# Where the weight sums of two matrices are made: block sums of w_out and w_proj_a moved into the recurrence and the attention

## The chip, the cores and the metric

The kernel runs on one core of a Trainium2 chip (8 cores, two dies of four). A core has five engines that run side by side, each with its own instruction queue: TensorE (PE) for matrix products, VectorE (DVE), ScalarE (ACT), GpSimd (POOL), and SyncE (SP), which here only issues transfers. Transfers (DMAs) are issued from the queues of SP, ACT and POOL and are carried out by 16 DMA engines. The metric is the device time of one execution in microseconds (us), lower is better.

## The reference

One decoder layer on 512 tokens of 1024 channels, float32, with two parallel branches:

```python
h = rms_norm(x, norm_g)
proj = h @ w_in                       # columns: recurrence q, f, i, gate z_a | attention c_q, c_kv, rope key, gate z_b | merge logits
y_a = hgrn2_branch(hq, hf, hi, hz, lower_bounds, hg_norm_g)     # gated linear recurrence, 8 heads of 128, chunks of 32
y_b = mla_branch(cq, ckv, kr, mz, q_a_g, w_uq, kv_a_g, w_ukv)   # latent attention, causal, 8 heads
gates = sigmoid(glog + b_gate)        # two gates of 1024 channels
merged = gates[0] * (y_a @ w_proj_a) + gates[1] * (y_b @ w_proj_b)
x = x + merged @ w_out
return rms_norm(x, final_norm_g)
```

## The kernel before

**Products.** Every float32 operand is split into a high part (a cast, on ACT) and the rest (a subtraction, on DVE), and a product is three matmuls: high by high, high by low, low by high. Weights come in blocks of 128 x 1024 numbers (512 KB): `load_w` issues the transfer on SP into one of three `w_raw` slots (L112), ACT casts it to `w_hi` (L118), DVE subtracts to `w_lo` (L119), four slots each. A transfer can only be issued when its slot is free, so SP waits for the `w_lo` of three blocks before.

**Strassen products.** The two merge gates (columns of `w_in`), `w_proj_a` and `w_out` are multiplied by a Strassen scheme with seven block products in place of eight. It needs four sums of 512 x 512 blocks of the weight. They are made by the DMA engines in DRAM by the class `BlockSums`: for each of the four sums, `start` queues two copies of 512 KB from the matrix into a DRAM tensor (`g_t`, `pa_t`, `out_t`; L751), and `add(n)` adds a second block to sum n by two accumulating DMAs on POOL's queue (L758). Sums 1 and 3 (`add(1)`, `add(3)`) add one of these tensors to another. `sum(n)` loads a finished sum through `load_w`, `block(i, j)` loads a block of the matrix itself.

The queued copies are not issued at once. Each `load_w` transfer that SP issues takes one copy from the list `queued` and issues it right behind itself. The adds on POOL are tied to POOL's work: `step()` takes the next entry of the list `adds` and places it behind POOL's latest instruction.

**Stages.** (1) norm of x, latent projections; (2) the recurrence, four pairs of heads (`hg_pair`), two or three calls of `step()` in a pair; (3) the attention, eight heads: scores, softmax (POOL scales the rows, L699), transposes on PE (L715), values; every second head there is a rotary exchange (`mla_turn`), in which ACT's queue moves rows between partitions by DMA (`qs<-qr`, L628 and L635) and POOL multiplies (L629 to L631); (4) the first merge gate by Strassen (`strassen`, matmuls L849), whose first two products run in head 7, then the second gate, then `w_proj_a`; (5) `w_proj_b` in four chunks of 256 columns; (6) `w_out` by Strassen (L1045), the residual sum, the final norm and the store.

Before the change, `start` is called for the two gates and `w_proj_a` ahead of the recurrence, and for `w_out` ahead of stage 4's remaining five products. The adds of `w_proj_a` are placed in heads 2 (two sums), 4 and 6, those of `w_out` behind the first gate's product. POOL also fetches there the stored sums of h (`s<-h`, L950), eight DMAs of 512 KB.

The order of instructions is made by a scheduler on all engines, except where `manual_schedule` keeps the written order: on PE in the Strassen products, and on PE, DVE and ACT in stage 6. The last Strassen product of `w_out` uses sum 4 (`t4`), which is loaded through `w_raw` and split into the tiles of sum 1 (`t_hl[0]`) once these are free.

Of the kernel before, what the change touches and what calls it, by code (L numbers as in the profile page):

```python
# [38 lines left out]
def hybrid_layer(ctx: ExitStack, tc: tile.TileContext, a):  # L39
    nc = tc.nc  # L40
# [117 lines left out]
    def split(hi, lo, src):  # L158

        nc.scalar.copy(hi, src)  # L160
        nc.vector.tensor_tensor(lo, src, hi.bitcast(F32), op=ALU.subtract)  # L161
# [460 lines left out]
    def mla_turn(pair):  # L622

        ps = low(load_w(w_uq[:, :, 2 * pair : 2 * pair + 2, 128:192]), 0, 3)
        qr, qs = ma_pool.tile([P, S], F32, "qr"), ma_pool.tile([P, S], F32, "qs")
        nc.scalar.copy(qr[:], ps[:])
        for b in range(4):
            nc.scalar.dma_start(qs[32 * b : 32 * b + 32, :], qr[32 * (b ^ 1) : 32 * (b ^ 1) + 32, :])  # L628
        nc.gpsimd.tensor_tensor(qr[:], qr[:], qtab[:, 0], op=ALU.mult)  # L629
        nc.gpsimd.tensor_tensor(qs[:], qs[:], qtab[:, 1], op=ALU.mult)  # L630
        nc.gpsimd.tensor_tensor(qr[:], qr[:], qs[:], op=ALU.add)  # L631

        qx = ma_pool.tile([P, S], F32, "qs")
        for i in range(2):
            nc.scalar.dma_start(qx[64 * i : 64 * i + 64, :], qr[64 - 64 * i : 128 - 64 * i, :])  # L635
        return qr, qx

    def mla_rope(qr, qx):

        qp, qh = [ma_pool.tile([P, S], F32R, f"qp{i}") for i in range(2)], ma_pool.tile([P, S], F32R, "qh")  # L640
        nc.scalar.copy(qh[:], qx[:])
        for i in range(2):
            own, other = slice(64 * i, 64 * i + 64), slice(64 - 64 * i, 128 - 64 * i)
            nc.scalar.copy(qp[i][own], qr[own])
            nc.vector.tensor_tensor(qp[i][other], qx[other], qh[other].bitcast(F32), op=ALU.subtract)
        return qp
# [34 lines left out]
    def mla_scores(h, pool, qn, kn, qp, final=False):  # L681

        pn = []
        for i in range(NT):
            n = (i + 1) * P
            bl = slice(i * P, n)
            sps = ax_tile()
            qh = qp[h % 2]
            mm3(sps[:, :n], qn, kn, (slice(None), bl), (slice(None), slice(0, n)), True, False)
            for x in range(2):  # L690
                nc.tensor.matmul(sps[:, :n], qh[:, bl], kpe[x][:, :n], start=False, stop=x == 1)  # L691
            sm = pool.tile([P, 4], F32, "sm", 4)
            p = pool.tile([P, n], F32, f"p{i}")
            nc.vector.tensor_tensor(sps[:, bl], sps[:, bl], mask_inf[:], op=ALU.add)
            nc.vector.tensor_reduce(sm[:, 0:1], sps[:, :n], axis=AX.X, op=ALU.max, negate=True)
            nc.vector.tensor_scalar(sm[:, 1:2], sm[:, 0:1], SCALE, None, op0=ALU.mult)  # L696
            nc.scalar.activation(p[:, :n], sps[:, :n], AF.Exp, scale=SCALE, bias=sm[:, 1:2], accum_out=sm[:, 2:3])  # L697
            nc.vector.reciprocal(sm[:, 3:4], sm[:, 2:3])
            scaled_p = (nc.vector if final else nc.gpsimd).tensor_scalar(p[:, :n], p[:, :n], sm[:, 3:4], 0.5,  # L699
                                                                         op0=ALU.mult, op1=ALU.mult)  # L700
            if not final:
                last_pool[0] = scaled_p
            pn.append(p)
        return pn
# [23 lines left out]
    kh = [slice(0, 2), slice(2, 4)]  # L728
# [40 lines left out]
    gate_w = [BlockSums(f"g{b}", w_in[:, COL_G + b * D : COL_G + b * D + D]) for b in range(2)]  # L769
    pa_w = BlockSums("pa", a["w_proj_a"][0])  # L770
    out_w = BlockSums("out", a["w_out"][0])
    h_dram = [[dram.tile([P, 4, 256], F32, name=f"h{n}{i}") for i in range(2)] for n in range(1, 5)]

    def early_sums(q):
# [9 lines left out]
        def keep(n, tag, src):  # L784
# [13 lines left out]
        keep(4, "qn", e12)  # L798

    adds = [(gate_w[0], 0), (gate_w[0], 2), (gate_w[1], 0), (gate_w[0], 1), (gate_w[1], 2), (gate_w[0], 3), (gate_w[1], 1),  # L800
            None, (gate_w[1], 3)]

    def step():
        if adds and last_pool[0]:
            x = adds.pop(0)
            if x:
                x[0].add(x[1])

    for w in (*gate_w, pa_w):
        w.start()  # L810

    for pair in range(H // 2 - 1):
# [93 lines left out]
    yb = ybp.tile([P, H, S], F32, "yb")  # L906
    qp, nope, pn = early
    late = None
    for h in range(H):
        pools = (ma_pool, mw)  # L910
        if h % 2 and h + 1 < H:
            turned_q = mla_turn((h + 1) // 2)
        if h:
            pn = mla_scores(h, pools[h % 2], *nope, qp, h + 1 == H)
        if h % 2 and h + 1 < H:
            qp = mla_rope(*turned_q)
        if h:
            z = mla_gate(h)
        if h:
            if h + 1 < H:  # L920
                nope = mla_nope(h + 1, pools[(h + 1) % 2])
            mla_out(*late)
            if h % 4 == 0:
                v = mla_values(h)
        hook = lambda: mla_transpose(pn)
        if h + 1 == H:
            with tc.manual_schedule(engines={mybir.EngineType.PE}):
                pts, later = [], []
                w11, w21 = gate_w[0].block(0, 0), gate_w[0].block(1, 0)
                u = ch_product(w11, h11, copied("c11", 1.0))  # L930
                ch_product(w21, h12, lambda b, ps: later.append((b, ps)), tile=mm_tile, hook=lambda: pts.extend(hook()))
                mla_out(h, pts, v, z)
        elif h:
            late = (h, hook(), v, z)
            if h % 2 == 0:
                pa_w.add(*{2: (0, 2), 4: (1,), 6: (3,)}[h])
        else:
            with tc.manual_schedule(engines={mybir.EngineType.PE}):
                nope = mla_nope(1, pools[1])
                v = mla_values(0)  # L940
                late = (0, hook(), v, z)
# [25 lines left out]
        closed("c11", 0, 0, 1.0, gate_out(0, lambda j: ma[:, j]))(b, ps)  # L967
    h_ops = (h11, h12, h22, s1, s2, s3, s4)
    y11, y12, y21, y22 = blocks(ya)
    out_w.start()  # L970
    with tc.manual_schedule(engines={mybir.EngineType.PE}):
        strassen(gate_w[0], h_ops, gate_out(0, lambda j: ma[:, j]), gp, first=u,
                 between={3: lambda: a_parts(y11, q1), 4: lambda: a_parts(y12, q2), 5: lambda: a_parts(y22, q3),
                          6: lambda: [minus(y22[:, q], y22[:, q], y21[:, q]) for q in kh]})
    out_w.add(0, 2)
    out_w.add(1)
    out_w.add(3)
    g1 = {j: z_tile()[:] for j in (0, 1, 4)}
    for n, j in enumerate((2, 3, 5, 6, 7)):
        g1[j] = g_rows[:, n]  # L980
# [28 lines left out]
    m_bot = [m2p.tile([P, 4, S], F32R, f"m_bot{i}") for i in range(2)]  # L1009
    t_hl = [[m2p.tile([P, 4, 512], F32R, f"t{n}{i}") for i in range(2)] for n in (1, 2)]  # L1010
    a11, a12, a21, a22 = blocks(ma)
    xr = [ya[:, 2 * t : 2 * t + 2].rearrange("p k c -> p (k c)") for t in range(NT)]
    for n, c in enumerate((0, 2, 1, 3)):
        for i, ps in enumerate(proj_ch(a["w_proj_b"][0], c * 256, ybs)):
            j = 2 * c + i
            g = g1[j]
            nc.vector.scalar_tensor_tensor(g, g, 1.0, ps[:], op0=ALU.add, op1=ALU.mult)
            nc.vector.tensor_tensor(ma[:, j], ma[:, j], g, op=ALU.add)
            if j < 4:
                split(m_top[0][:, j], m_top[1][:, j], ma[:, j, 0:256])  # L1020
            else:
                split(m_bot[0][:, j - 4], m_bot[1][:, j - 4], ma[:, j])
        if n == 1:
            t1 = out_w.sum(1, t_hl[0])
        elif n == 2:
            t2 = out_w.sum(2, t_hl[1])
            with tc.issue_after(last_dma[0].ins):
                for t in range(NT):
                    xr_in = nc.sync.dma_start(xr[t], a["x"][0, t * P : t * P + P, :])
    gp.close()  # L1030


# [106 lines left out]
    with tc.manual_schedule(engines={mybir.EngineType.PE, mybir.EngineType.DVE, mybir.EngineType.Activation}):  # L1139
        for q in kh:  # L1140
            minus(a22[:, q], a22[:, q], a21[:, q])
            split(s1[0][:, q], s1[1][:, q], a22[:, q])
        for q in kh:
            minus_minus(a22[:, q], a22[:, q], a11[:, q])
            split(s2[0][:, q], s2[1][:, q], a22[:, q])
        u = product(m_top, 0, w11, lambda t, ps: add_to(t, 0, ps), by_tile=False)
        for q in kh:
            minus_minus(a12[:, q], a12[:, q], a22[:, q])
        w22 = out_w.block(1, 1)
        product(m_bot, 0, w21, row11, tile=mm_tile, by_tile=False)  # L1150
        for q in kh:
            minus(a21[:, q], a11[:, q], a21[:, q])
        a_parts(a21, m_top)
        r = product(s1, 0, t1, lambda t, ps: add_to(t + 2, 1, ps), by_tile=False)
        a_parts(a12, s1)
        t3 = out_w.sum(3)
        product(s2, 0, t2, lambda t, ps: add_to(t, 1, ps), u, by_tile=False)
        t4 = out_w.sum(4, t_hl[0])
        product(s1, 0, w22, row12, r)
        product(m_top, 0, t3, row22, u)  # L1160
        last_product(m_bot, 2, t4, u, row21)
# [44 lines left out]
```

## Time and profile before

| | |
|---|---|
| three runs | 643.65, 645.54, 647.35 us; median 645.54 |
| profiled execution | 642.71 us; span from first to last instruction 640.8 us |
| PE busy | 609.8 us, 95% of the span |
| DVE, ACT, POOL busy | 433.1, 285.6, 147.0 us |
| mean granted clock of PE | 0.982 |
| moved by DMA | 114.37 MB, 178 GB/s in the mean |

In the groups of the profile, `out<-in` names the tile written and the tiles read, L is the line of the kernel, and x the count. In PE's, DVE's, ACT's and POOL's rows of the timeline the first number is the start in us from the span's start, the second the time of the row, and a bracket at the end tells how long the engine had been idle before it and what it waited for. "SPq" and "POOLq" stand for a queue that issues DMAs; the time of such a row is that of issuing, not of moving.

### The profile page before, as it was taken

What the parts mean: (1) busy time and instruction counts of PE and PEld (TensorE: products, weight loads), DVE (VectorE), ACT (ScalarE), POOL (GpSimd) and SP (SyncE); (2) the same over time, 40 slices, a digit from 0 to 9 for tenths busy, and PEclk for the clock granted to TensorE, in tenths of its full rate; (3) what the DMA queues carried; (4) which work ended last, traced back from release to release, by engine and by line L of the source; (5) the groups of instructions that cost most, each with busy time, mean ns of one, the idle gap of its engine ahead of it and who ended that gap; (6) DMA issues with size and microseconds to landing.
All of it is one profiled execution on the core that took longest, in us unless ns stands there. A gap on an engine that the chain in (4) does not pass through costs nothing.

```text
span 640.8 us, 9797 instructions
## 1 busy us (share of the span) xinstructions
PE 609.8 (95%) x3688; PEld 533.7 (83%) x3688; DVE 433.1 (68%) x679; ACT 285.6 (45%) x531; POOL 147.0 (23%) x245
## 2 busy tenths in 40 slices
PE   8999999999999999999989999947799999999994
PEld 5998888888888888888878888947799999888883
DVE  7727989498945479675767667523467777667785
ACT  5554343333233333355445545342467864333352
POOL 3106322535422045113441142401100000000002
PEclk9999999999999999999999999987899999999999
DMA  7549399969695523504393825999976555685123
GB/s 258 165 139 339 115 296 339 265 180 218 197 210 125 142 71 86 134 16 117 74 192 77 177 82 131 344 278 255 209 225 187 181 192 174 194 319 147 59 98 132
DMA packets 74799, 114.37 MB, mean 178 GB/s; under 512 B 7512, under 2 KB 41726, under 8 KB 74752
## 3 DMA queue, kind: packets, MB, share of 16 engines
q1 hardware_dynamic: 65100, 89.69, 44.1%
q0 software_dynamic: 7952, 21.50, 17.8%
q10 hardware_dynamic: 1700, 2.56, 1.4%
q8 instruction: 29, 0.48, 0.3%
q14 instruction: 18, 0.15, 0.1%
HBM read 105.34 MB, written 39.85 MB: 227 GB/s over the span
## 4 chain that ended last, share of the span: by engine, by line
PE 80%; DMA 7%; DVE 5%; ACT 3%; issue 2%; POOL 2%; ACTq 1%; POOLq 0%; DVEq 0%
PE mm_ps L91 17%; PE mm_ps L92 17%; PE mm_ps L93 17%; PE ax_ps L849 14%; DMA w_raw<-w_in 3%; PE mm_ps L849 3%; DMA w_raw<-g_t 2%; DMA qs<-qr 2%; PE mm_ps L271 1%; PE ax_ps L691 1%; DVE w_lo L119 1%; PE ax_ps L541 1%; PE ax_ps L715 1%; PE ax_ps L236 1%; PE ax_ps L503 1%
## 5 line engine op out<-in xcount | busy, mean ns | idle before, releaser
L119 DVE TENSOR_TENSOR w_lo<-w_raw,w_hi 128x1024 fp32r<-128x1024 f32 (+3 forms) x116 | 138.4, 1204 | 109.0 <-ACT w_hi L118 103.1
L118 ACT CAST w_hi<-w_raw 128x1024 fp32r<-128x1024 f32 (+3 forms) x116 | 115.4, 1005 | 168.9 <-PE mm_ps L92 75.5
L91 PE MATMUL mm_ps<-hT,w_hi 128*128 128x512 f32 x320 | 125.7, 394 | 0.3 <-DVE qn L161 0.3
L92 PE MATMUL mm_ps<-hT,w_hi 128*128 128x512 f32 x320 | 125.1, 391 | 0.0
L93 PE MATMUL mm_ps<-hT,w_lo 128*128 128x512 f32 x320 | 124.7, 392 | 0.0
L849 PE MATMUL ax_ps<-s,w_hi 128*128 128x256 f32 x384 | 59.8, 301 | 16.0 <-ACT w_hi L118 16.0
L91 PEld LDWEIGHTS mm_ps<-hT,w_hi 128*128 128x128 f32 x320 | 60.1, 188 | 12.3 <-DVE qn L161 0.6
L93 PEld LDWEIGHTS mm_ps<-hT,w_lo 128*128 128x128 f32 x320 | 60.1, 188 | 12.3
L92 PEld LDWEIGHTS mm_ps<-hT,w_hi 128*128 128x128 f32 x320 | 60.1, 188 | 11.8
L849 PEld LDWEIGHTS ax_ps<-s,w_hi 128*128 128x128 f32 x384 | 54.6, 209 | 16.8 <-ACT w_hi L118 16.8
L93 PE MATMUL mm_ps<-w_hi,hT 128*128 128x512 f32 (+1 forms) x96 | 36.6, 383 | 0.0
L92 PE MATMUL mm_ps<-w_lo,hT 128*128 128x512 f32 (+1 forms) x96 | 36.5, 382 | 0.0
L91 PE MATMUL mm_ps<-w_hi,hT 128*128 128x512 f32 (+1 forms) x96 | 36.4, 386 | 0.0
L1096 POOL TENSOR_SCALAR ssum<-ssum 128x1 f32<-128x1 f32 x3 | 0.9, 310 | 154.3 <-ACT sq L1083 154.3
L849 PE MATMUL ax_ps<-s,w_lo 128*128 128x256 f32 x192 | 33.2, 297 | 0.0
L699 POOL TENSOR_SCALAR p<-p,sm 128x128 f32<-128x128 f32 (+3 forms) x28 | 15.2, 545 | 65.5 <-DVE sm L696 33.2
L849 PEld LDWEIGHTS ax_ps<-s,w_lo 128*128 128x128 f32 x192 | 28.6, 206 | 0.2 <-DVE w_lo L119 0.2
L697 ACT ACTIVATE p<-ax_ps,sm 128x128 f32<-128x128 f32 (+3 forms) x32 | 16.9, 529 | 25.6 <-DVE sm L696 23.3
L460 DVE RECIPROCAL tf<-pr 128x512 f32<-128x512 f32 x8 | 26.8, 3349 | 0.2
L91 PE MATMUL mm_ps<-cT,w_hi 128*128 128x512 f32 x52 | 20.7, 398 | 0.0
L93 PEld LDWEIGHTS mm_ps<-w_hi,hT 128*128 128x128 f32 x96 | 18.0, 188 | 3.0
L91 PEld LDWEIGHTS mm_ps<-w_hi,hT 128*128 128x128 f32 x96 | 18.0, 188 | 3.0
(296 smaller groups left out, 1207.8 us busy)
## 6 DMA issues: line engine op xcount, KB each, us to landing
w_raw<-w_in SPq DMA_DIRECT2D x54, 512.0 KB, 5.5
g_t<-w_in SPq DMA_DIRECT2D x16, 512.0 KB, 8.6
w_raw<-g_t SPq DMA_DIRECT2D x16, 512.0 KB, 4.7
g_t<-w_in POOLq DMA_DIRECT2D x8, 512.0 KB, 9.9
pa_t<-w_proj_a SPq DMA_DIRECT2D x8, 512.0 KB, 12.9
g_t<-g_t POOLq DMA_DIRECT2D x8, 512.0 KB, 10.2
out_t<-w_out SPq DMA_DIRECT2D x8, 512.0 KB, 17.3
s<-h POOLq DMA_DIRECT2D x8, 512.0 KB, 10.5
```

The lines of the kernel that those rows point to most:

```text
L91: nc.tensor.matmul(ps, lh[lsl], rh[rsl], start=start, stop=False)
L92: nc.tensor.matmul(ps, lh[lsl], rl[rsl], start=False, stop=False)
L93: nc.tensor.matmul(ps, ll[lsl], rh[rsl], start=False, stop=stop)
L118: last_hi[0] = nc.scalar.copy(hi[:, :o], raw[:, :o])
L119: last_lo[0] = nc.vector.tensor_tensor(lo[:, :o], raw[:, :o], hi[:, :o].bitcast(F32), op=ALU.subtract)
L236: nc.tensor.matmul(idle[:], zero[:, :P], zero[:], start=True, stop=True)
L271: nc.tensor.matmul(ps, hT[l][:, 4 * kh + k, t * P : t * P + P], c_hl[kh][r][:, k * 256 : k * 256 + 256], start=kh == 0 and kind == 0 and k ...
L460: nc.vector.reciprocal(rp[:], pr[:])
L503: nc.tensor.matmul(sps[:, sl], kt_[:, sl], v_sb[i][:, (h % 4) * P : (h % 4) * P + P], start=True, stop=True)
L697: nc.scalar.activation(p[:, :n], sps[:, :n], AF.Exp, scale=SCALE, bias=sm[:, 1:2], accum_out=sm[:, 2:3])
L699: scaled_p = (nc.vector if final else nc.gpsimd).tensor_scalar(p[:, :n], p[:, :n], sm[:, 3:4], 0.5, op0=ALU.mult, op1=ALU.mult)
L849: nc.tensor.matmul(ps[:, o], w[k // 2][i][:, k % 2, cols], ap[j][:, k], start=not banks and c == 0 and n == 0, stop=n == 11, skip_group_ch ...
```

## The change

```diff
     adds = [(gate_w[0], 0), (gate_w[0], 2), (gate_w[1], 0), (gate_w[0], 1), (gate_w[1], 2), (gate_w[0], 3), (gate_w[1], 1),
-            None, (gate_w[1], 3)]
+            (pa_w, 0), (gate_w[1], 3), (pa_w, 2), None, (pa_w, 1), (out_w, 0), (pa_w, 3), (out_w, 2), (out_w, 1), (out_w, 3)]
...
-    for w in (*gate_w, pa_w):
+    for w in (*gate_w, pa_w, out_w):
         w.start()
...
             late = (h, hook(), v, z)
-            if h % 2 == 0:
-                pa_w.add(*{2: (0, 2), 4: (1,), 6: (3,)}[h])
+            step()
...
-    out_w.start()
     with tc.manual_schedule(engines={mybir.EngineType.PE}):
         strassen(gate_w[0], h_ops, gate_out(0, lambda j: ma[:, j]), gp, first=u,
...
-    out_w.add(0, 2)
-    out_w.add(1)
-    out_w.add(3)
...
+    t4_raw = yb[:, 4:8]
...
                     xr_in = nc.sync.dma_start(xr[t], a["x"][0, t * P : t * P + P, :])
+                for q in kh:
+                    xr_in = nc.sync.dma_start(t4_raw[:, q], out_w.t[3][:, q])
...
-        t4 = out_w.sum(4, t_hl[0])
+        t4 = [[t[:, q] for t in t_hl[0]] for q in kh]
+        for hl, q in zip(t4, kh):
+            split(*hl, t4_raw[:, q])
```

Three things change. The copies of `w_out` are queued with the others ahead of the recurrence, so that they come out behind loads of head pairs 2 and 3. The adds of `w_proj_a` and `w_out` go into the list of `step()`, one sum at a time: two in pairs 2 and 3, and one in each of heads 1 to 6, where `step()` is now called. Sum 4 of `w_out` is no longer loaded through the `w_raw` slots near the end, but by two DMAs into the upper half of `yb`, the second branch's output, which is read for the last time in stage 4; they are issued in stage 5 behind the loads of x.

How this moves instructions is shown at three places. First SP, in head pairs 2 and 3, as a piece of the difference (`pa_t_658` is the last of w_proj_a's four tensors, `out_t_659` and `out_t_660` the first two of w_out's):

```order
 L751 DMA pa_t_658<-w_proj_a 128x2x512
-L112 DMA w_raw<-w_in 128x4x256 x2
+L112 DMA w_raw<-w_in 128x4x256
+L751 DMA out_t_659<-w_out 128x2x512
+L112 DMA w_raw<-w_in 128x4x256
+L751 DMA out_t_659<-w_out 128x2x512
 L110 DMA w_raw<-w_uq 128x2x64 x3
-L112 DMA w_raw<-w_in 128x4x256 x6
+L112 DMA w_raw<-w_in 128x4x256
+L751 DMA out_t_660<-w_out 128x2x512
```

Each of eight loads there now has a copy of w_out behind it; the same eight copies are gone from behind the loads of the first gate.

Second POOL, in heads 4 to 6. Before:

```order
L699 TENSOR_SCALAR p_3522<-p_3522,sm 128x512
L758 DMA pa_t_656<-pa_t_655 128x1024 x2
L699 TENSOR_SCALAR p_3719<-p_3719,sm 128x128
L699 TENSOR_SCALAR p_3733<-p_3733,sm 128x256
L699 TENSOR_SCALAR p_3747<-p_3747,sm 128x384
L629 TENSOR_TENSOR qr<-qr,qtab 128x512
L630 TENSOR_TENSOR qs<-qs,qtab 128x512
L699 TENSOR_SCALAR p_3761<-p_3761,sm 128x512
L631 TENSOR_TENSOR qr<-qr,qs 128x512
L699 TENSOR_SCALAR p_3888<-p_3888,sm 128x128
```

And with the change:

```order
L699 TENSOR_SCALAR p_3536<-p_3536,sm 128x512
L758 DMA out_t_661<-w_out 128x2x512 x2
L699 TENSOR_SCALAR p_3733<-p_3733,sm 128x128
L699 TENSOR_SCALAR p_3747<-p_3747,sm 128x256
L699 TENSOR_SCALAR p_3761<-p_3761,sm 128x384
L699 TENSOR_SCALAR p_3775<-p_3775,sm 128x512
L758 DMA out_t_660<-out_t_659 128x1024 x2
L629 TENSOR_TENSOR qr<-qr,qtab 128x512
L630 TENSOR_TENSOR qs<-qs,qtab 128x512
L631 TENSOR_TENSOR qr<-qr,qs 128x512
L699 TENSOR_SCALAR p_3904<-p_3904,sm 128x128
```

Head 4's sum is now one of w_out, head 5 has a sum of its own ahead of the rotary products, and its last scaling has moved ahead of them.

Third ACT, in the first gate (`part` is the copy of a product's banks, `q` a part of the recurrence's output that is split there). Before:

```order
L160 CAST q_4342<-ya 128x512 x2
L865 ACTIVATE part<-ax_ps 128x512 x2
L118 CAST w_hi<-w_raw 128x1024 x2
L160 CAST q_4344<-ya 128x512 x2
L118 CAST w_hi<-w_raw 128x1024
L865 ACTIVATE part<-ax_ps 128x512
L118 CAST w_hi<-w_raw 128x1024
```

And with the change:

```order
L160 CAST q_4358<-ya 128x512 x2
L865 ACTIVATE part<-ax_ps 128x512
L118 CAST w_hi<-w_raw 128x1024 x2
L160 CAST q_4360<-ya 128x512 x2
L865 ACTIVATE part<-ax_ps 128x512
L118 CAST w_hi<-w_raw 128x1024 x2
L160 CAST q_4362<-ya 128x512 x2
```

The casts of the next product's two blocks stood behind both copies of the banks; now they stand between the two.

## The prediction

> **What bounds the kernel now.** I read the page first, then the stages by windows, the idle gaps of TensorE (PE) row by row, the chain of waits, and last the transfers.
>
> ```profile
> span 640.8 us, 9797 instructions
> ...
> PE   8999999999999999999989999947799999999994
> ...
> PEclk9999999999999999999999999987899999999999
> ```
>
> One slice is 16 us. PE is full nearly everywhere, except for the last slice and a dip (4, 7, 7) at slices 27 to 29, from 416 us on; there the granted clock dips too. Stage by stage (from:to, length, busy us of PE, PEld, DVE, ACT, POOL, then clock, share of the DMA engines, GB/s):
>
> ```profile
> 80.00:120.00 40.00, 40.00 (x266) 33.70 (x266) 30.47 (x46) 17.13 (x37) 10.59 (x9) 1.00 1.01 314
> 160.00:230.00 70.00, 70.00 (x445) 59.54 (x438) 40.21 (x52) 24.06 (x57) 21.97 (x33) 1.00 0.66 160
> 230.00:400.00 170.00, 166.68 (x932) 142.15 (x931) 121.14 (x250) 78.95 (x175) 51.11 (x77) 1.00 0.46 107
> 421.77:463.60 41.83, 25.04 (x145) 24.06 (x145) 14.22 (x17) 13.76 (x20) 5.61 (x6) 0.76 1.01 248
> 480.00:540.00 60.00, 60.00 (x503) 60.00 (x502) 44.04 (x56) 42.47 (x64) 0.00 (x0) 1.00 0.57 186
> ```
>
> The fourth row is the first merge gate's Strassen product, the fifth the same kind of work for the second gate and w_proj_a. There PE does 503 matmuls in 60 us, 119 ns each, with the DMA engines at 0.57. In the fourth row three products of 48 matmuls need 41.83 us, and the DMA engines are full (1.01). PE's own rows show the gaps, with what ended each in brackets:
>
> ```profile
> 421.13 0.64 PE L849 MATMUL ax_ps<-s,w_lo 128*128 128x256 f32 x4
> 423.39 0.50 PE L849 MATMUL ax_ps<-s,w_hi 128*128 128x256 f32 x2 [1.62 <-ACT w_hi L118]
> 431.32 1.65 PE L849 MATMUL ax_ps<-s,w_hi 128*128 128x256 f32 x6 [7.43 <-ACT w_hi L118]
> ...
> 444.14 1.65 PE L849 MATMUL ax_ps<-s,w_hi 128*128 128x256 f32 x6 [4.49 <-ACT w_hi L118]
> ...
> 455.26 0.98 PE L849 MATMUL ax_ps<-s,w_hi 128*128 128x256 f32 x6 [2.42 <-ACT w_hi L118]
> ...
> 463.60 1.18 PE L849 MATMUL ax_ps<-hT,w_hi 128*128 128x256 f32 x8 [0.79 <-DVE part L872]
> ```
>
> PE waits for the cast of a weight block; the chain says what the cast waited for:
>
> ```profile
> 424.62 18.34 DMA w_raw<-w_in
> 443.04 1.05 ACT w_hi L118
> 445.37 15.08 DMA w_raw<-g_t
> ```
>
> So two loads set the end of this stage. The transfers of 421 to 464 us and, below, of 480 to 540 us (count, size, median us to landing):
>
> ```profile
> out_t<-out_t POOLq DMA_DIRECT2D x4, 512.0 KB, 9.6
> w_raw<-g_t SPq DMA_DIRECT2D x4, 512.0 KB, 12.4
> w_raw<-w_in SPq DMA_DIRECT2D x3, 512.0 KB, 13.7
> out_t<-w_out SPq DMA_DIRECT2D x3, 512.0 KB, 18.0
> ...
> w_raw<-g_t SPq DMA_DIRECT2D x4, 512.0 KB, 4.2
> ```
>
> The same load takes 12.4 us beside the copies and sums of w_out, and 4.2 us without them. A block of 24 matmuls lasts 2.9 us on PE and there are three raw slots, so landing, the cast of 1.05 and the subtraction after it, about as long, must fit into 8.6 us: with 4.2 they do, with 12.4 they don't.
>
> **Part 1: the eight copies and eight sums of w_out leave the first gate.** Without late loads the three products take 3 x 48 x 0.12 = 17.28 us. The stage loses 41.83 - 17.28 = 24.55 us: 16.79 idle, and 25.04 - 17.28 = 7.76 of matmuls at the lower clock. Both go when the loads are on time. The order of ACT supports it: the two casts of the second product stood behind both copies of the first one's banks (the 1.62 us gap), and now stand between them. Bounds of what remains: nothing, or the whole 1.62 us plus its share of slow clock; the load issued last before the stage stays close to its need, so I take half, 0.8. Gain 23.7 us.
>
> The slow part can be weighed. "TensorE: Matmul & The Clock Gate" of the Trainium skill (Part 1: The HAM clock gate) says that an idle window of about 3.4 us halves PE's clock and about 3.4 us of sustained work restores it. Three gaps would by that cost at most 3 x 1.7 = 5.1 us, and the sum would be 2.7 us smaller; the 7.76 us of the rows decide.
>
> **Part 2: the copies now ride behind the loads of head pairs 2 and 3, from about 164 us.** Each adds 512 KB read and written. I cost this at nothing: from 80 to 120 us such copies already run, the engines are as full as in the bad stage (1.01), and PE is busy 40.00 of 40.00: a block's 24 matmuls on 512 columns last 5.3 us there (0.22 us each, by the row 565:575 in part 4), against 2.9 in the gates. Where they go the share is 0.66. If the cover were gone, rival D has the price.
>
> **Part 3: the sums, one at a time.** Two of w_proj_a's go to pair 2 and 3, the others and w_out's four go one to each of heads 1 to 6. Each is two DMAs on POOL's queue, in front of the softmax scalings (L699) that PE's transposes (L715) wait for.
>
> ```profile
> 315.88 4.70 POOL L758 DMA_DIRECT2D pa_t<-w_proj_a  x4
> ...
> 344.00 0.37 POOL L699 TENSOR_SCALAR p<-p,sm 128x128 f32<-128x128 f32 x1 [8.10 <-DVE sm L698]
> ...
> 352.07 1.70 POOL L758 DMA_DIRECT2D pa_t<-pa_t  x2
> ...
> 373.07 2.25 POOL L631 TENSOR_TENSOR qr<-qr,qs 128x512 f32<-128x512 f32 x1
> 387.03 0.37 POOL L699 TENSOR_SCALAR p<-p,sm 128x128 f32<-128x128 f32 x1 [11.71 <-DVE sm L696]
> ...
> PE ax_ps L715 <- POOL p L699: 2.4, 2, 1.6
> ```
>
> Head 2 issues two DMAs (2.4 us) where it issued four (4.70). Head 3's fall into idle time of 8.10 us. Head 4 pays 2.4 for 1.70. Head 5's 1.70 stands ahead of the rotary products (L629 to L631), with 11.71 us idle behind them. No sum waits for an unfinished one: each comes at least a head after what it reads, some 21 us here (387.03 - 344.00 is two heads), against 9.6 us of landing. So 0, between a gain of the 2.4 us that PE waits there now and a loss as large.
>
> **Part 4: the last block's sum goes to the yb tile early.** Its two loads no longer hold ACT and DVE at the end:
>
> ```profile
> 620.28 1.05 ACT L118 CAST t<-w_raw 128x1024 fp32r<-128x1024 f32 x1 [4.09 <-DMA w_raw<-out_t]
> ...
> 627.34 5.87 PE L1045 MATMUL ax_ps<-t,m_bot 128*128 128x512 f32 x36 [0.93 <-DVE ya L1079]
> ...
> 547.18 0.40 PE L91 MATMUL mm_ps<-hT,w_hi 128*128 128x512 f32 x1
> ...
> 565.00:575.00 10.00, 10.00 (x45) 8.28 (x45) 5.98 (x9) 1.97 (x3) 0.00 (x0) 1.00 1.02 378
> ...
> 576.12 1.05 ACT L118 CAST w_hi<-w_raw 128x1024 fp32r<-128x1024 f32 x1 [3.96 <-DMA w_raw<-w_proj_b]
> ```
>
> DVE stands in order, so the late second half pushes the row sums behind it, and PE's last product waits 0.93 us for one; that goes, and since only that product's own epilogue follows, the end moves with it. Bounds: 0 and 0.93. The price is 1 MB more at 565 us, at 378 GB/s 2.8 us, ahead of w_proj_b's last two loads. Their cast moves from 576.1 to about 579; PE reaches them after three chunks of 48 matmuls at 10.00/45 = 0.22 us and 24 short ones, 547.2 + 32.0 + 2.9 = 582 us. Covered; uncovered it would cost up to 2.8.
>
> **Sum.** 23.7 + 0 + 0 + 0.9 = 24.6 us. The profiled execution took 642.71 us, 1.9 more than its span, so it would take 618.1. It lies 2.8 us under the median of the runs, 645.54; from that, 621 us is my forecast.
>
> **Rivals.**
>
> B, half of the stall stays. The loads into the first gate also run beside the fetch of the h sums. Those of 385 to 421 us landed like this:
>
> ```profile
> L112 SPq DMA_DIRECT2D w_raw<-g_t x4: 327/334/347, 390.6 to 416.0; - x4
> ...
> DMA to landing us min/median/max: 4.4/9.3/14.2
> ```
>
> If two loads stay 9.3 - 4.2 = 5.1 us late, 10.2 us of idle and, at 7.76/16.79, 4.7 of slow clock remain: 621 + 14 = 635. Against it: the engines stay full through all of 421 to 464 us, and the list of that time shows no such fetch.
>
> C, the sums disturb the rotary exchange. Its hops, ACT's DMAs qs<-qr, lie on the chain:
>
> ```profile
> 289.33 3.50 DMA qs<-qr
> ...
> 323.18 6.17 DMA qs<-qr
> ```
>
> The second ran beside four sums, the first beside none. If each of the three exchanges has both hops 2.7 us longer and PE pays all, 16 us come back: 637. For it: more sums lie in the attention now, twelve DMAs for eight; "DMA: Bandwidth & Descriptors" of the Trainium skill (Issuing engines are not separate DMA queues) says that transfers of every engine share the same 16 and interleave, and these two rows agree. Against it: PE idles only 3.3 us in all of 230 to 400 us (third row of the windows), with eight such DMAs, and head 2 loses two.
>
> D, slower: SP's queue is held by the copies in pair 2 and 3. Loads queue behind them on SP, and one copy's issue already took long (the first row: least, median and most ns of one):
>
> ```profile
> L751 SPq DMA_DIRECT2D pa_t<-w_proj_a x8: 564/686/10022, 109.4 to 154.0; - x8
> ...
> 187.09 26.04 SPq L112 DMA_DIRECT2D w_raw<-w_in  x6
> ...
> 198.12 1.05 ACT L118 CAST w_hi<-w_raw 128x1024 fp32r<-128x1024 f32 x1 [1.84 <-PE mm_ps L92]
> ```
>
> If all eight take 10.02 us against PE's 5.3 per block, PE falls 8 x 4.7 = 38 us behind. A load's lead, from its issue to the cast that waits only for PE, covers 198.1 - 187.1 - 4.2 = 6.8; 31 us are lost for 24.6 gained: 652. It decides from (24.6 + 6.8)/8 + 5.3 = 9.2 us per copy. Against it: w_proj_a's eight took 0.7 us in the median, and PE never stopped.
>
> That the scheduler leaves the copies where they were is excluded by the order.
>
> **How the numbers follow.** Forecast 0.72; B 0.12; C 0.08; B and C together, near 649 and with any cushion about where it was, 0.03; D 0.05. 0.5% is 3.2 us, about what a measurement of this kernel can tell from no change. Faster: 0.72 + 0.12 + 0.08 = 0.92; within 0.03; slower 0.05. The likeliest case alone runs from 645.5 - 24.55 - 0.93 - 2.4 = 617.7, less 1.9 of spread in the runs, to 621 + 1.6 + 0.9 + 2.4 + 2.8 = 629. Leaving out no more than 2 in 10, the range is 615 to 634.
>
> **What would show it.** In the changed profile: part 1 is right if the three products between the first and the last of the gate take under 20 us at clock 1.00, with loads landing in 4 to 6 us; part 2 if PE stays full from 160 to 230 us; part 3 if PE's idle time from 230 to 400 us stays under 6 us; part 4 if the last product no longer waits. Loads landing above 9 us in the first gate without any copy beside them would make part 1 wrong, a gap of PE between 164 and 250 us part 2.

## The result, and the profile after

The changed kernel takes 622.74 us in the median of four runs (621.24 to 625.46), the kernel before in the same comparison 644.6 us (640.87 to 647.35): a ratio of 0.967, 95% interval 0.961 to 0.973. Forecast were 621.0 us and a range of 615 to 634. The profiled execution took 623.33 us against 642.71 before, 19.4 us less, where the sum of the prediction's terms was 24.6. The total is near; but one of its terms is larger than what the whole gained, and two that were put at nothing took 5.7 us back.

The page of the changed kernel (span, then PE and the granted clock in 40 slices of 15.5 us):

```profile
span 621.4 us, 9796 instructions
...
PE   8999999999999998999998999999999999999995
...
PEclk9999999999999998999999999999999999999998
```

The dip of slices 27 to 29 is gone; the granted clock has a new, small one in slice 16, at 245 us (told under The clock). The stages by windows of the changed kernel (length, busy PE, PEld, DVE, ACT, POOL, clock, share of the DMA engines, GB/s); the third row holds the gate's three products that took 41.83 us before:

```profile
160.00:230.00 70.00, 70.00 (x452) 59.58 (x446) 39.09 (x50) 22.32 (x54) 20.75 (x32) 1.00 0.82 219
230.00:400.00 170.00, 164.49 (x905) 139.41 (x904) 116.45 (x238) 77.47 (x170) 61.21 (x87) 0.99 0.58 124
427.48:445.76 18.28, 17.79 (x146) 17.38 (x145) 14.63 (x17) 12.61 (x20) 0.00 (x0) 1.00 0.67 208
480.00:540.00 60.00, 60.00 (x472) 58.63 (x471) 43.25 (x58) 35.13 (x50) 0.00 (x0) 1.00 0.58 182
```

The loads issued in those 18 us (count, size, median us to landing):

```profile
w_raw<-w_in SPq DMA_DIRECT2D x4, 512.0 KB, 4.9
w_raw<-g_t SPq DMA_DIRECT2D x4, 512.0 KB, 4.9
```

PE's own rows, with what it waited for in brackets: in pair 3 of the recurrence, the last scores of pair 3 (L517), the gate's first product, two waits in the gate, and the last product of w_out:

```profile
244.25 0.50 PE L91 MATMUL mm_ps<-hT,w_hi 128*128 128x512 f32 x1 [1.99 <-DVE z L563]
...
263.34 0.86 PE L517 MATMUL ax_ps<-qi,ki 128*64 128x64 f32 x22
...
407.19 1.16 PE L849 MATMUL ax_ps<-hT,w_hi 128*128 128x256 f32 x8
...
428.13 0.98 PE L849 MATMUL ax_ps<-s,w_hi 128*128 128x256 f32 x6 [0.25 <-ACT w_hi L118]
...
429.58 0.51 PE L849 MATMUL ax_ps<-s,w_lo 128*128 128x256 f32 x2 [0.24 <-DVE w_lo L119]
...
608.36 5.78 PE L1043 MATMUL ax_ps<-t,m_bot 128*128 128x512 f32 x36
```

With five landmarks of PE the 19.4 us are placed: the start of the last scores of pair 2 and of pair 3 (L517), of the first gate's first product and of the product of its last sum (the rows `ax_ps<-hT` of L849), and of the last product of w_out. Each row of the table ends at the landmark that it names.

| stretch | before | after | difference | prediction |
|---|---|---|---|---|
| start to pair 2's scores | 211.19 | 211.33 | +0.14 | 0 |
| to pair 3's scores (259.29; 263.34) | 48.10 | 52.01 | +3.91 | 0 |
| to the first gate (401.31; 407.19) | 142.02 | 143.85 | +1.83 | 0 |
| to the product of the gate's last sum (463.60; 445.76) | 62.29 | 38.57 | -23.72 | -23.7 |
| to w_out's last product (627.34; 608.36) | 163.74 | 162.60 | -1.14 | -0.9 |
| to the end of the span | 13.46 | 13.04 | -0.42 | 0 |

The gate's gain is as forecast to a tenth. New is the loss in pair 3, where PE waits 1.99 us for a gate value z of the recurrence, and a smaller one in the attention.

### The profile page after: what moved, and what is told of

It reads as the page before. It is cut to its first block, busy times and chain, and to the rows that moved or that the text cites. A ratio compares the mean times of both kernels' runs of the same rounds, so it can differ in the third digit from the quotient of the medians.

```text
span 621.4 us, 9796 instructions
## 1 busy us (share of the span) xinstructions
PE 604.7 (97%) x3688; PEld 528.3 (85%) x3688; DVE 431.7 (69%) x679; ACT 285.2 (46%) x531; POOL 147.6 (24%) x245
## 4 chain that ended last, share of the span: by engine, by line
PE 69%; DVE 10%; DMA 8%; ACT 5%; issue 4%; POOL 2%; ACTq 1%; POOLq 0%; SPq 0%; DVEq 0%
PE ax_ps L849 16%; PE mm_ps L91 13%; PE mm_ps L92 13%; PE mm_ps L93 13%; PE mm_ps L849 3%; DVE w_lo L119 3%; DMA w_raw<-w_proj_b 2%; DMA w_raw<-w_uq 2%; ACT w_hi L118 2%; PE mm_ps L271 2%; DMA qs<-qr 1%; DMA w_raw<-out_t 1%; DMA w_raw<-w_out 1%; DVE ya L1077 1%; PE ax_ps L691 1%
## 5 line engine op out<-in xcount | busy, mean ns | idle before, releaser
L119 DVE TENSOR_TENSOR w_lo<-w_raw,w_hi 128x1024 fp32r<-128x1024 f32 (+3 forms) x116 | 136.7, 1190 | 98.5 <-ACT w_hi L118 92.8
L849 PE MATMUL ax_ps<-s,w_hi 128*128 128x256 f32 x384 | 54.1, 283 | 0.2 <-ACT w_hi L118 0.2
L849 PEld LDWEIGHTS ax_ps<-s,w_hi 128*128 128x128 f32 x384 | 49.6, 192 | 0.5 <-ACT w_hi L118 0.5
L849 PE MATMUL ax_ps<-s,w_lo 128*128 128x256 f32 x192 | 31.3, 284 | 0.2 <-DVE w_lo L119 0.2
L849 PEld LDWEIGHTS ax_ps<-s,w_lo 128*128 128x128 f32 x192 | 26.6, 192 | 0.4 <-DVE w_lo L119 0.4
L457 POOL TENSOR_SCALAR k<-tf,c1n,c 128x512 f32<-128x512 f32 x8 | 16.0, 1995 | 26.6 <-ACT tf L454 26.6
L93 PEld LDWEIGHTS mm_ps<-w_hi,hT 128*128 128x128 f32 x96 | 18.0, 188 | 3.0
```

Source lines behind the costliest of these rows:

```text
L93: nc.tensor.matmul(ps, ll[lsl], rh[rsl], start=False, stop=stop)
L119: last_lo[0] = nc.vector.tensor_tensor(lo[:, :o], raw[:, :o], hi[:, :o].bitcast(F32), op=ALU.subtract)
L457: nc.gpsimd.tensor_scalar(k[:], tf[:], c1n[:, h : h + 1], c1[:, h : h + 1], op0=ALU.mult, op1=ALU.add)
L849: nc.tensor.matmul(ps[:, o], w[k // 2][i][:, k % 2, cols], ap[j][:, k], start=not banks and c == 0 and n == 0, stop=n == 11, skip_group_ch ...
```

## The experiments

**Pair 3: the sum on POOL, or the copies?** The z that PE waits for stands behind a reciprocal on DVE, and that behind a scan that needs `fr` from POOL. POOL's rows in the changed kernel:

```profile
227.83 1.27 POOL L631 TENSOR_TENSOR qr<-qr,qs 128x512 f32<-128x512 f32 x1
229.07 2.03 POOL L166 TENSOR_TENSOR ss<-ss,fixed 128x4 f32<-128x4 f32 x2
231.07 2.40 POOL L758 DMA_DIRECT2D pa_t<-w_proj_a  x2
232.61 2.76 POOL L457 TENSOR_SCALAR k<-tf,c1n,c 128x512 f32<-128x512 f32 x1
235.45 0.62 POOL L456 TENSOR_SCALAR fr<-f 128x16 f32<-128x16 f32 x1
```

The two issues of w_proj_a's first sum stand in the middle, and `fr` comes at 235.45 us; before it came at 231.04. My first theory (T1) was that sum. The edit moves it one slot on:

```diff
-            (pa_w, 0), (gate_w[1], 3), (pa_w, 2), None, (pa_w, 1), ...
+            None, (gate_w[1], 3), (pa_w, 0), (pa_w, 2), (pa_w, 1), ...
```

> The first sum of w_proj_a moves from the end of pair 2 to the next slot, in pair 3; the other sums keep their order and no work is left out. Theory T1 (that sum's two DMA issues, 2.4 us on POOL, stand in front of pair 3's k and fr, which DVE's scan and through it z wait for): PE's wait for z at 244 us is gone or under 0.5 us, no 512-column matmul near it lasts 0.43 us, and pair 3's last scores stand at 259 to 260 us, as before the change, where the changed kernel has 263.3; the whole is 3.5 to 4 us shorter than the changed kernel, about 618.5 to 620. Rival T2 (the copies of w_out or the transfers of the sum itself slow pair 3): the copies stand where they were, so the wait and the slow matmuls stay, pair 3's scores at 262 to 264 us, and the time is the changed kernel's within 1 us.

Beside it ran the changed kernel once more:

> The changed kernel once more, unedited, so that the other runs of this call stand beside it on the same chip. Every theory expects 621 to 625 us, PE's wait for z at about 244 us in pair 3 (2 us) with eight 512-column matmuls at about 0.43 us behind it, and the first product of the first gate at about 407 us.

The changed kernel took 623.6 us (0.970 of before, 0.968 to 0.973), the edit 621.55 (0.967, 0.9645 to 0.969). T1 failed: pair 3's scores stood at 261.65 and 261.31 us, and PE still waited 1.44 us where the changed kernel, run again, waits 2.20. POOL's and PE's rows of the edit:

```profile
225.16 1.29 POOL L629 TENSOR_TENSOR qr<-qr,qtab 128x512 f32<-128x512 f32 x1 [20.54 <-DMA qs<-qr]
...
228.97 1.28 POOL L631 TENSOR_TENSOR qr<-qr,qs 128x512 f32<-128x512 f32 x1
230.22 2.03 POOL L166 TENSOR_TENSOR ss<-ss,fixed 128x4 f32<-128x4 f32 x2
232.26 0.77 POOL L457 TENSOR_SCALAR k<-tf,c1n,c 128x512 f32<-128x512 f32 x1
233.52 0.28 POOL L456 TENSOR_SCALAR fr<-f 128x16 f32<-128x16 f32 x1 [0.49 <-DVE f L455]
...
243.62 0.50 PE L91 MATMUL mm_ps<-hT,w_hi 128*128 128x512 f32 x1 [1.44 <-ACT tf L454]
```

No sum stands there now, and `fr` is still 2.5 us later than before the change, because POOL's rotary products, ahead of it in the queue, end later: the first, L629, starts at 225.16 us, before the change at 222.68. It waits for the first hop of the rotary exchange (`qs<-qr`). The hop's four DMAs in the window of 206 to 232 us (median us to landing), in the kernel before, then in the edit together with the copies in flight there:

```profile
qs<-qr ACTq DMA_DIRECT2D x4, 64.0 KB, 2.6
```

```profile
out_t<-w_out SPq DMA_DIRECT2D x2, 512.0 KB, 10.6
qs<-qr ACTq DMA_DIRECT2D x4, 64.0 KB, 5.2
```

The copies of w_out make the hop 2.6 us later. So the next edit let the copies start eleven loads later, from about 235 us, with the first sum where the change had put it (`copies_late`), and with that sum one slot later as well (`both_late`):

```diff
-    for w in (*gate_w, pa_w, out_w):
+    for w in (*gate_w, pa_w):
         w.start()
+    queued.extend([lambda: None] * 11)
+    out_w.start()
```

> The changed kernel with the copies of w_out eleven loads later, so that they run from about 235 us, behind pair 2's rotary exchange; the sum of w_proj_a stays at the end of pair 2. Theory T1+2 (pair 3's gap of 2 us has two causes: the exchange's hops land 2 us later beside the copies, and the sum's 2.4 us on POOL stand before k and fr): the hops take 2.4 to 3 us again, the gap shrinks to 0.5 to 1.5 us and stays above nothing. Theory T1 (the sum alone): hops or not, the gap stays at 2 us. Theory T2 (the copies alone): the gap goes, pair 3's scores at 259.3 us.

> The same with the first sum of w_proj_a also one slot later. Theory T1+2: no gap over 0.3 us at 244 us, pair 3's scores at 259 to 259.5 us as before the change, time 619 to 620.5 us, 2 to 2.5 under the changed kernel. Theory T2: the same as the run with the copies late. A third cause (for example the later stretch of the copies meeting pair 3's own loads): a gap of over 0.5 us remains somewhere between 230 and 300 us and the time stays at 621 to 623.

The hop took 2.7 us in both. With the copies late PE does not wait 0.3 us anywhere near 244 us, and pair 3's scores start at 259.86 us although the sum's two issues are still there; with both, at 259.24, as before the change:

```profile
259.86 1.15 PE L517 MATMUL ax_ps<-qi,ki 128*64 128x64 f32 x32
```

So T2 was nearly right: the copies alone cost 2.0 us (261.31 against 259.29), the sum alone 0.6 (259.86 against 259.24), and both 1.8 to 2.6 (261.05 to 261.85 in the five further profiles in which both stand, without the slow matmuls told of next). Together they cost at most the sum of the two: both delay the same chain.

**The clock.** In the first profile of the change the scores came at 263.34, 1.7 us later still, after a gap no longer than in the second. Its windows there (columns as above; the clock is the third number from the end):

```profile
241.97:245.38 3.41, 1.42 (x7) 0.95 (x6) 3.41 (x7) 1.69 (x3) 0.98 (x1) 1.00 0.32 95
245.38:248.79 3.41, 3.41 (x10) 2.66 (x9) 1.86 (x3) 0.34 (x1) 3.04 (x3) 0.50 0.38 104
```

and of the same kernel's second profile, whose gap was 2.20 us:

```profile
240.46:243.88 3.42, 1.54 (x7) 0.94 (x5) 3.42 (x4) 0.24 (x1) 0.00 (x0) 1.00 0.33 78
243.88:247.29 3.41, 3.09 (x14) 2.56 (x15) 3.06 (x5) 1.79 (x3) 2.95 (x1) 1.00 0.52 154
```

The trace records the clock in steps of whole multiples of 3.41 us, and I cut these windows on that grid. In the first execution the whole gap fell into one step, PE was busy for 42% of it, and the next step ran at half the clock; in the second the gap straddled a boundary, PE was busy for 45%, and the clock stayed. Over the steps from 195 to 600 us of 14 profiles, of those that ran at full clock with PE busy for under 44% all 14 were followed by a step at half, and of those from 55% to 75% none; between lies a mixture (from 45% to 55%, 6 of 13). "TensorE: Matmul & The Clock Gate" of the Trainium skill (Part 1: The HAM clock gate) tells of a free-running window of 3.4 us, and the trace agrees with its steps of 3.41. It also says that an idle window of that length is what halves the clock; here a gap of 1.99 us was enough when it fell into one step.

The repair earned little. `copies_late` took 621.42 us over five further runs (0.968, 0.966 to 0.970), and `both_late` 621.91 (0.9695, 0.9665 to 0.9725), where 619 to 620.5 had been expected:

> The kernel with the copies eleven loads later, timed in rounds: in its one look pair 3's gap was gone (scores at 259.9 us instead of 261.7 to 263.3). If that gap is the only thing that moves, it takes 1.8 to 3.5 us less than the changed kernel (ratio to before 0.9645 to 0.967); if a half-clock window in the attention comes with it, as in its one look, the 1.7 us are given back and the ratio is the changed kernel's, 0.967 to 0.970.

In all three profiles of the two kernels a step at half clock came back in the attention. That of `both_late`, where PE waits 0.74 and 1.36 us for POOL's softmax rows:

```profile
334.65:338.06 3.41, 1.65 (x9) 1.28 (x10) 0.00 (x0) 0.60 (x1) 3.41 (x6) 1.00 0.46 125
338.06:341.47 3.41, 3.41 (x16) 3.31 (x15) 2.09 (x4) 3.35 (x8) 1.02 (x2) 0.50 0.92 169
```

Nearly the same two waits (0.70 and 1.35 us) stood in the changed kernel and cost no clock there. So a step at half clock, worth up to 1.7 us, took back most of what pair 3 had gained. No version that I ran is clearly better than the change: the intervals of 621.4 to 621.9 us and of 622.7 and 623.6 overlap.

**More copies.** Eight further copies of 512 KB, that nothing reads, behind those of w_out:

```diff
+    more_w = BlockSums("more", a["w_out"][0])
...
-    for w in (*gate_w, pa_w, out_w):
+    for w in (*gate_w, pa_w, out_w, more_w):
```

> The changed kernel with eight further 512 KB copies (extra work that nothing reads) queued behind those of w_out in the recurrence, so they run from the last stretch of pair 3 on and into the first heads. Theory P (the copies are free where PE does 512-column blocks, since those last 5.3 us): pair 2's last scores stay at 211 us, the end moves by under 1.5 us. Rival D of the prediction (SP's queue is held by copies and loads queue behind them): each copy beyond what the lead covers costs up to 4.7 us, so at least 5 us longer by the first gate (first product at 412 us or later instead of 407).

PE was busy 70.00 of 70.00 us from 160 to 230, pair 2's scores at 211.05, pair 3's at 261.19, the gate's first product at 407.19 us, as in the changed kernel, and the time of its one run 623.27 us. The median issue on SP stayed at 0.56 us for w_out's and 0.73 us for the further ones. Rival D, SP's queue held by the copies, is excluded up to twice their number.

**What made the loads late in the gate?** Copies alone, eight that nothing reads, queued at the gate of the changed kernel:

```diff
+    more_w = BlockSums("more", a["w_out"][0])
...
     y11, y12, y21, y22 = blocks(ya)
+    more_w.start()
     with tc.manual_schedule(engines={mybir.EngineType.PE}):
```

> The changed kernel with eight further 512 KB copies inside DRAM (extra work that nothing reads) queued at the first gate, where the copies of w_out stood before; no sums there. Theory P (the prediction: loads that share the DMA engines with copies and sums land late): copies alone are 8 MB read and written of the 14.7 MB that copies and sums brought, so a good half of the stall returns: the three products of the gate take 28 to 38 us where the changed kernel has 19 to 20, with w_raw landing in 8 to 12 us. Rival Q (the accumulating sums are what slows the loads, plain copies share fairly): three products within 2 us of the changed kernel's, w_raw landing under 7 us.

The stretch from the gate's first product to that of its last sum (38.57 us in the changed kernel, 62.29 before), with the length first, then the two queues' packets, MB and share of the engines' time in it (q1 holds the loads and copies, q0 the fetch of the h sums):

```profile
406.74:448.87 42.13, 40.02 (x312) 39.18 (x312) 24.21 (x34) 22.98 (x38) 3.82 (x8) 0.96 0.92 304
...
q1 hardware_dynamic: 3661, 8.59, 61.9%
q0 software_dynamic: 1155, 4.19, 29.4%
```

This run brings back 3.6 us of 23.7, much less than I expected, and none of it is a late load. PE's only waits of over 0.1 us in the stretch, and ACT's rows ahead of them:

```profile
428.83 0.50 PE L850 MATMUL ax_ps<-s,w_hi 128*128 128x256 f32 x2 [1.62 <-ACT w_hi L118]
429.78 1.51 PE L850 MATMUL ax_ps<-s,w_hi 128*128 128x256 f32 x6 [0.45 <-ACT w_hi L118]
...
427.25 0.60 ACT L866 ACTIVATE part<-ax_ps 128x512 f32<-128x512 f32 x1 [2.22 <-PE ax_ps L850]
427.74 1.98 ACT L118 CAST w_hi<-w_raw 128x1024 fp32r<-128x1024 f32 x2
```

The scheduler has put both casts behind both copies of the banks again, as before the change, and they run back to back, so their blocks had landed. A step at half clock, worth up to 1.7 us, follows; that and 1.6 us more of idle time make up nearly all of the 3.6. The loads landed in 4.0 us (`w_raw<-w_in`) and 5.7 (`w_raw<-g_t`). So the copies alone cost PE no wait for a load here, and the order of the casts is worth up to 3.6 us. The same wait of 1.62 us behind that order stands before the change and in the next three runs.

Then four sums alone, which nothing reads, with their copies early as in the run with more copies:

```diff
                           6: lambda: [minus(y22[:, q], y22[:, q], y21[:, q]) for q in kh]})
+    more_w.add(0, 2)
+    more_w.add(1)
+    more_w.add(3)
```

> The run with eight further copies early (more_copies), and beside them four further sums (eight accumulating DMAs on POOL, extra work that nothing reads) behind the first gate's product, where the sums of w_out stood before; no copy runs in the gate. The eight copies alone at the gate brought back 3.5 us of the 23.7. Theory Q (the sums are what made the loads late): first gate, from its first product to that of the last sum's block, 53 to 62 us instead of 38.6, w_raw landing in 10 us or more. Theory P (copies and sums only together fill the DMA engines long enough): 39 to 44 us, w_raw landing under 8 us, and the sums' own end is just earlier.

The stretch took 57.25 us and the run 640.79, but it tells something else: the sums got in front of the fetch of the h sums on POOL's queue, and PE waited for that fetch:

```profile
432.12 1.19 PE L850 MATMUL ax_ps<-s,w_hi 128*128 128x256 f32 x4 [11.45 <-DMA s<-h]
```

So the sums of w_out themselves were taken out of the heads and tied behind the fetch, first with the copies left in the recurrence (from `both_late`), then with these at the gate too (`out_w.start()` back where it stood before):

```diff
-            None, (gate_w[1], 3), (pa_w, 0), (pa_w, 2), (pa_w, 1), (out_w, 0), (pa_w, 3), (out_w, 2), (out_w, 1), (out_w, 3)]
+            None, (gate_w[1], 3), (pa_w, 0), (pa_w, 2), (pa_w, 1), None, (pa_w, 3)]
...
-            nc.gpsimd.dma_start(s[i][:], h_dram[n - 1][i][:])
+            last_pool[0] = nc.gpsimd.dma_start(s[i][:], h_dram[n - 1][i][:])
...
+    out_w.add(0, 2)
+    out_w.add(1)
+    out_w.add(3)
```

> The run with copies and first sum late (both_late), and the four sums of w_out taken out of heads 1 to 6 and issued in the first gate behind the fetch of the h sums, where in before they met the copies; the copies stay in the recurrence. At the gate: if the sums alone make the loads late, the stretch from its first product to that of the last sum's block (38.6 us in the changed kernel, 62.3 before, 42.1 with copies alone) takes 48 us or more; if copies and sums only together do, 38.6 to 43 us. In the attention: if the sums of w_out in the heads are what lengthened it (from pair 3's scores to the gate 142.0 us before, 143.6 to 145.1 since, with the half-clock windows left out), 142 to 143 us here, and the time is 617 to 619 with a free gate; if the changed order of ACT and DVE does it whatever POOL issues, 144 us or more, and 619 to 622.

> The same, but the eight copies of w_out back at the first gate too, so that it differs from the run above only in the place of the copies. If the two together fill the DMA engines and so delay the loads (the prediction's reason), the stretch takes 58 to 64 us again with w_raw landing in about 12 us, and the time is 638 to 642 us. If the prediction's stall came from something else that the change moved (the order of ACT's casts, the queue of POOL ahead of the h sums), it takes under 50.

The same stretch of the two kernels; a late load of the first, by PE's wait and the cast that it waits for; and the transfers of its bad part (423 to 456 us) with the queues' MB and share of the engines' time (q0 holds the sums, q1 the loads):

```profile
402.91:455.77 52.86, 44.76 (x319) 44.01 (x318) 24.69 (x33) 22.25 (x36) 12.35 (x16) 0.87 0.97 256
```

```profile
399.66:460.36 60.70, 45.12 (x319) 43.97 (x318) 24.14 (x34) 21.49 (x36) 12.46 (x16) 0.86 0.99 262
```

```profile
441.73 1.65 PE L851 MATMUL ax_ps<-s,w_hi 128*128 128x256 f32 x6 [4.74 <-ACT w_hi L118]
...
440.63 1.04 ACT L118 CAST w_hi<-w_raw 128x1024 fp32r<-128x1024 f32 x1 [6.70 <-DMA w_raw<-w_in]
```

```profile
q0 software_dynamic: 1219, 3.32, 57.9%
q1 hardware_dynamic: 1720, 4.47, 38.6%
...
out_t<-out_t POOLq DMA_DIRECT2D x4, 512.0 KB, 12.3
w_raw<-w_in SPq DMA_DIRECT2D x4, 512.0 KB, 7.9
w_raw<-g_t SPq DMA_DIRECT2D x4, 512.0 KB, 10.4
```

That makes a table of four (the idle time is the length less PE's busy time in the row of windows):

| at the gate | stretch | PE idle in it | clock |
|---|---|---|---|
| neither (the changed kernel) | 38.57 | 0.49 | 1.00 |
| copies alone | 42.13 | 2.11 | 0.96 |
| sums alone | 52.86 | 8.10 | 0.87 |
| both | 60.70 | 15.58 | 0.86 |
| before the change | 62.29 | 16.79 | 0.84 |

In the runs with the sums eight short matmuls of head 7 fell behind the gate's first product, about 1.0 us, which are no stall. Without these the sums alone bring back 13.3 us, both 21.1, and 2.6 us of the 23.7 stay unexplained. All but the first kernel have the old order of casts, up to 3.6 us by the run with copies alone. So sums make loads late by themselves; copies, which alone make none late enough for PE to wait, add another 7.8 us beside them. The queues' rows show why a sum weighs more than its bytes: its 3.32 MB kept the 16 engines for 57.9% of 33 us, 92 us of one engine for each MB; the loads' 4.47 MB 38.6%, 46 us. Neither POOL's queue nor plain copying is that dear: in the 42.13 us of the run with copies alone the fetch on POOL's queue took 47 us for each MB, and the loads and copies together 49. With the sums at the gate the time is 634.36 us (0.9865, 0.982 to 0.991), with both 639.94 in one run.

**One sum at a time beside the second gate**, each started behind a row of gate outputs, where PE is full and the engines are at 0.6 (the sums are out of the heads as above):

```diff
+    seen = gp.tile([P, 4], F32, "seen")
+
+    def add_behind(col, x, n):
+        last_pool[0] = nc.gpsimd.tensor_copy(seen[:, col : col + 1], x)
+        out_w.add(n)
+
+    add_behind(0, ma[:, 3, 511:512], 0)
...
+    add_behind(1, g1[3][:, 0:1], 1)
+    add_behind(2, g1[6][:, 0:1], 3)
+    add_behind(3, g1[3][:, 511:512], 2)
```

> The run with copies and first sum late (both_late), and the four sums of w_out taken out of the heads and spread over the second gate, each started behind a row of gate outputs (about 450, 462, 479 and 491 us), one at a time. The engines are at 0.60 there with PE full, and a sum of 1 MB kept all 16 engines busy for about 5.3 us (69.2% of 30 us for 3.93 MB where the sums ran alone on their queue), so one in 16 us brings the share to about 0.93. Theory A (a load is late only where several sums are under way together): PE stays full from 440 to 540 us, attention from pair 3's scores to the gate 140.5 to 142 us, time 616 to 618.5, better than the changed kernel. Theory B (every sum makes the loads beside it late by its own engine time): each costs 2 to 4 us as in the first gate (14.3 us for four), time 626 to 634.

Theory B held in the main: 635.6 us (0.991, 0.987 to 0.994), 1.6 over its range. From 450 to 520 us the gate's loads (`w_raw<-g_t`) landed in 9.6 us where the changed kernel has 4.1. PE, full from 440 to 540 us in the changed kernel, idles 8.77 us there and loses 5% of its clock:

```profile
440.00:540.00 100.00, 91.23 (x719) 90.26 (x718) 61.31 (x77) 56.13 (x87) 9.89 (x12) 0.95 0.75 201
```

Three of the four sums were followed by a wait of PE (1.00, 3.69 and 4.05 us), the third, started at 490 us, by none. The share does not say it: at 0.75 there is room in the mean, and still a load beside a sum can be late. A block lasts 2.9 us on PE in these products. In the heads, where the change has its sums, they cost far less; that this is for the fewer loads there was not tested by itself.

**The attention** stayed open. From pair 3's scores to the gate it took 142.0 us before and 143.6 to 145.0 in the five profiles with the sums in the heads and no step at half clock. Without w_out's sums in the heads it took 143.5, 144.1 and 140.3 (`sums_after_h`, `sums_gate2`, `both_at_gate`). The first two have a step at half clock, worth up to 1.7 us, and all three lack the 1.0 us of head 7 that went behind the boundary. Put right for both, they run from 141.3 to about 143.4. The sums may cost 1 or 2 us there; the order of DVE and ACT, which the scheduler chose anew in these kernels, may do as much, and no run holds one of the two fixed.

**The last block** fetched through the load slots again (part 4 undone):

```diff
-                for q in kh:
-                    xr_in = nc.sync.dma_start(t4_raw[:, q], out_w.t[3][:, q])
...
-        t4 = [[t[:, q] for t in t_hl[0]] for q in kh]
-        for hl, q in zip(t4, kh):
-            split(*hl, t4_raw[:, q])
+        t4 = out_w.sum(4, t_hl[0])
```

> The changed kernel without its second part: the last block of w_out is fetched at the end through the load slots again, as before the change. The prediction's part 4: PE's last product waits 0.93 us for a row sum again and the end is 0.9 us later, measured from the first gate's fourth product on. If the 1.6 us that the tail got shorter has another cause, the wait does not return, or only part of it.

The wait is back with 0.81 us, and from the gate's first product to w_out's last it takes 202.14 us against 201.17 in the changed kernel and 201.16 in its second profile, 0.97 us:

```profile
607.63 5.86 PE L1041 MATMUL ax_ps<-t,m_bot 128*128 128x512 f32 x36 [0.81 <-DVE ya L1075]
```

## Why the prediction was right, and where not

**Part 1** held in size and in its means: 18.28 us for the three products instead of 41.83, clock 1.00, loads landing in 4.9 us, the residue 18.28 - 17.28 = 1.0 us where 0.8 was taken. Its cause was too coarse. Copies and sums were counted as one thing that fills the DMA engines. Of the 21.1 us that both bring back, the sums alone bring 13.3; the copies alone made PE wait for no load. The order of the casts, which the prediction took only as a support and as the bound of what remains, is worth up to 3.6 us by itself, and both figures have it in them. The prediction weighed the clock's loss by a page of the Trainium skill, "TensorE: Matmul & The Clock Gate" (Part 1: The HAM clock gate), at an estimate of at most 5.1 us for three gaps, against 7.76 from the rows. The rows were right: in the kernel before, the gate has three stretches at half clock, 10.24, 6.83 and 3.41 us. Steps there at half clock with PE busy for 0, 55% and 80% were followed by another, so a stall could cost more than one step.

**Part 2** is the step that failed. It looked at PE in the stage in which the copies run, from 160 to 230 us, where PE indeed stays at 70.00 of 70.00 us, and costed them at nothing. The last copies overlap pair 2's rotary exchange, whose first hop lands 1.9 to 2.6 us later (4.5 to 5.2 instead of 2.6), and PE feels it 20 us afterwards, at 244 us. The copies alone cost 2.0 us there, and one profile of the change lost 1.7 of clock on top. The prediction had named the gap that would show it, "a gap of PE between 164 and 250 us". Rival C was this mechanism, but put on the sums in three exchanges of the attention, at 16 us. By copies, in the one exchange of the recurrence that they meet, it was real. "DMA: Bandwidth & Descriptors" of the Trainium skill (Issuing engines are not separate DMA queues), which was cited there, says that DMAs interleave on the same 16 engines whichever engine issues them. The hop's rows agree: ACT's four DMAs took 4.5 to 5.2 us beside SP's copies, and 2.6 to 2.7 without.

**Part 3** costed the heads only and left out the sum that the change sets at the end of pair 2. Alone it costs 0.6 us. For the heads it took 0 within 2.4 either way; measured were 1.8, inside the bound, with the cause unsettled. PE's idle time from 230 to 400 us is 5.5 us, under the 6 that were named, but 2.2 more than before, most of it the gap of part 2.

**Part 4** was 0.93 by the wait and is 0.97 by its undoing. The tail got shorter by a further 0.6 us (1.56 in all), which has not been traced.

**Rivals.** B (half the stall stays) did not happen: the waits left are 0.25 and 0.24 us. D is excluded by the run with twice the copies. That the total came within 2 us of the forecast is owed to part 1, and in part to luck. The terms at zero were 5.7 us wrong, in the direction that was priced as a rival, and the profiled execution took 623.33 us where the sum gave 618.1, 5.2 more. The forecast had added 2.8 us because the profiled execution before lay under the median of its runs; the changed kernel's lay 0.6 over its own.

## What to carry to other kernels

Ask of a background transfer not only whether the stage it runs in keeps PE full, but which small transfer on a chain it overlaps: a hop of 64 KB lost 2.6 us beside copies of 512 KB, and the bill came 20 us later on another engine. Accumulating sums are the dear part of such work: a low mean share of the DMA engines is no sign that they fit beside weight loads on a tight chain, and here the attention took them far more cheaply than the gates. Look also at what a scheduler does with the other engines' order when transfers move: the order of two casts was worth up to 3.6 us here. And count a gap of PE of about 2 us with its possible step at half clock, which comes or not by chance of position.

## What the hardware showed that was not expected

A sum made by the DMA engines took 92 us of one engine for each MB, a plain load 46, and one sum at a time was enough to make loads of the gate land in 9.6 instead of 4.1 us with the engines at a mean share of 0.75. The granted clock changed on a fixed grid of 3.41 us, and in these 14 profiles it went by how busy PE was in the step before. Of the steps at full clock, all 14 with PE busy for under 44% were followed by a step at half, and from 45% to 55% 6 of 13 were. A step at half clock was followed by one at full only where PE was busy for 90% of it or more; in all 11 with 80% or less the clock stayed down. So one and the same kernel with a gap of 2.0 or 2.2 us in the same place lost 1.7 us of clock in one execution and nothing in the other.
